# Moving the low parts of two weight blocks behind the activations' work, and finishing the norms' column halves one by one

## The chip, the cores and the metric

One core of a Trainium2 chip runs the whole program in one launch. The metric is device time in microseconds from launch to end, the median of several executions. Engines named below: PE is TensorE (matmuls and transposes), PEld its weight loads, DVE is VectorE, ACT is ScalarE, POOL is GpSimd, SP is the queue that issues nearly all of the loads.

## The reference, cut to what matters

256 tokens of width 1024 pass through four layers (first block), then through two more of another kind, which the change does not touch. The part of a layer that the change touches:

```python
        y = mixer(h)                                  # attention of one of three kinds, ends in @ w_out
        x = x + rmsnorm(y, g[1])
        y = sqrelu_mlp(rmsnorm(x, g[2]), mlp_w1[i], mlp_w2[i])   # square(relu(h @ w1)) @ w2, 1024 -> 4096 -> 1024
        x = x + rmsnorm(y, g[3])
        x = x + jax.nn.sigmoid(x @ ple_gate_w[i]) * (p[i] @ ple_w[i])
```

All of it is in fp32. The kernel keeps that accuracy with three passes of a faster type: each operand a is split in a high part (rounded to `fp32r`) and a low part (a minus the high part), and a product is high x high + low x high + high x low.

## The kernel before, in words

**Pieces of weights.** A weight block of 512 rows by 512 columns (1 MB) is loaded by SP into a buffer `raw`; ACT casts it into `whi` (the high part); DVE subtracts in two instructions of 128 x 1024 to give `wlo` (the low part, `rest`, L289). There are four buffers of each of the three names. A `raw` buffer is free for the next load only when the low part has been taken from it. `piece` does cast and subtraction together (cast at L270); `high` and `low` do them apart (cast at L277). Column block 0 of the MLP's first weights and of the gate's weights is made by `high` and `low`; each consists of two pieces, k = 0 and k = 1.

**Activations.** `transpose_in` turns 128 tokens of x into operands with the features on the partitions: four transposes on PE for each column half, then ACT writes the high part (`xTh`) and DVE the low part (`xTl`, both L423).

**End of a mixer (`first_layer`).** `mixed` multiplies the mixer's output by w_out, tokens 0 to 127 first (`y`), then tokens 128 to 255 (`y1`, through `begin` and `end`). DVE forms `gg` and `xg` (L2192, L2196) from x and the norms' weights. `enter(y, h)` finds the norm of y (squares on ACT, a chain of small DVE instructions), and for each column half multiplies (L2202) and adds (L2203) to give xg[h], the unnormalised input of the MLP. The order in the program is: enter(y, 0); the end of y1; the cast of the small weight `ple_w`; `high` and `low` of the MLP's first block; transposes of xg[0]; `ple_in` (transposes of p); enter(y1, 1); `ple_proj` (p @ ple_w on PE, its results kept in one of the `raw` buffers until the layer ends); transposes of xg[1]; then `update`, which adds the normed y to x itself (L2208, L2209, eight instructions); then the MLP. The MLP's column block 0 goes through `mm_a4` (L342): all of its high x high matmuls, then all low x high, then all high x low. After it the blocks alternate between `mm_a` and the product with w2 (`mm_b`); the w2 pieces of block 0 and the w1 pieces of block 1 come through the four `raw` buffers in that order.

**End of a layer.** `post_norm` norms the MLP's output Y[h] and adds it to x[h], again multiply (L457) and add (L458) for each column half. The gate's two column blocks `ug` are made by `unit_apart` (block 0) and `unit` (block 1). Then, for h = 0 and 1: transposes of x[h], and the gate matmuls `mm_b`, column block 0 before block 1, in each for k = 0 and k = 1: high x high, low x high, high x low.

**What sets the order.** The program order above is a ranking. The compiler keeps a timeline of its own and gives each engine's queue the highest ranked instruction whose operands are ready in that timeline, some instructions ahead of the one that executes; the queue then runs in that order on the chip. `with self.behind(done)` adds order alone: what is traced inside on the engine of `done` stands behind `done` in that engine's queue, and does not wait for it to end. `self.weighted` is the mixer's last multiplication on DVE. The SP queue is in order too: a load that waits for a buffer holds those behind it.

Of the kernel before, what the change touches and what calls it, by code (L numbers as in the profile page):

```python
# [16 lines left out]
OP = mybir.AluOpType  # L17
# [35 lines left out]
class Net:  # L53
# [239 lines left out]

        return [self.piece(w[k * 512:(k + 1) * 512, c0:c0 + nc_], 4 * k, perm) for k in range(2)]

    def unit_apart(self, w, c0):

        raws = [self.load(w[k * 512:(k + 1) * 512, c0:c0 + 512]) for k in range(2)]
        u = [self.high(raw, 4 * k) for k, raw in enumerate(raws)]
        for p, raw in zip(u, raws):  # L300
            self.low(p, raw)
        return u


# [145 lines left out]
    def post_norm(self, y, g, h, r2):  # L450

        v = self.nc.vector
        r4 = self.small([128, 1], "r4")
        v.tensor_scalar(r4, r2, r2, 1.0 / D, op0=OP.mult, op1=OP.mult)
        r = self.rstd(y, scale=r4, factor=r2)
        for n, yn in zip(HALVES, y):
            v.scalar_tensor_tensor(yn, yn, r, g[:, n], op0=OP.mult, op1=OP.mult)  # L457
            last = v.tensor_add(self.x[h][:, n], self.x[h][:, n], yn)  # L458
        return last


# [1714 lines left out]
    def first_layer(self, i, mix, oT, w_out, after):  # L2176
        nc, v = self.nc, self.nc.vector
        ng = self.a["norm_g"][i]
        xg, r2 = {}, {}
        y, begin, end = self.mixed(mix, oT, w_out)  # L2180
        raws = [self.load(self.a["mlp_w1"][i, k * 512:(k + 1) * 512, :512]) for k in range(2)]
        mT = self.xT_new()
        if i == 3:
            self.pools = ExitStack()
            self.rt = self.pools.enter_context(self.tc.tile_pool(name="rt", bufs=1, reuse_waits="tile"))
        with self.phase(f"mlp{i}", 4, 4):

            g1, g2 = self.bcast(ng[1]), self.bcast(ng[2])
            gg = self.tm()

            with self.behind(self.weighted):
                v.tensor_tensor(gg, g1, g2, OP.mult)  # L2192
                for h in range(2):
                    xg[h] = self.tm()
                    for n in HALVES:
                        v.tensor_tensor(xg[h][:, n], self.x[h][:, n], g2[:, n], OP.mult)  # L2196

            def enter(y, h):
                r = self.rstd(y)
                for n, yn in zip(HALVES, y):  # L2200
                    t = self.t2([128, 512])
                    v.scalar_tensor_tensor(t, yn, r, gg[:, n], op0=OP.mult, op1=OP.mult)  # L2202
                    v.tensor_add(xg[h][:, n], xg[h][:, n], t)  # L2203
                return r

            def update(y, h, r):
                for n, yn in zip(HALVES, y):
                    v.scalar_tensor_tensor(yn, yn, r, g1[:, n], op0=OP.mult, op1=OP.mult)  # L2208
                    v.tensor_add(self.x[h][:, n], self.x[h][:, n], yn)  # L2209
                r = self.rstd([self.x[h]])  # L2210
                r2[h] = self.one([128, 1], f"r2{h}")
                v.tensor_tensor(r2[h], r, r, OP.mult)

            r0 = enter(y, 0)
            y1 = begin()
            for u in range(2):
                end(y1, u)
            pc = self.piece(self.a["ple_w"][i])
            u1 = [self.high(raw, 4 * k) for k, raw in enumerate(raws)]
            with self.behind(self.weighted):  # L2220
                for u, raw in zip(u1, raws):
                    self.low(u, raw)
            self.transpose_in(xg[0], mT, 0)
            pT = self.ple_in(i)
            r1 = enter(y1, 1)
            self.ple_proj(pc, pT)
            last = self.transpose_in(xg[1], mT, 1)
            with self.behind(*last):
                update(y, 0, r0)
                update(y1, 1, r1)  # L2230
            g3 = self.bcast(ng[3])
            Y, last = self.mlp(i, mT, u1)
            if i == 3:
                self.router_loads()
            xT = self.xT_new()
            y = [self.wide(), self.wide()]
            self.post_norm(Y[0], g3, 0, r2[0])
            with self.behind(*last):
                ug = [self.unit_apart(self.a["ple_gate_w"][i], 0)]
            for h in range(2):  # L2240
                last = self.transpose_in(self.x[h], xT, h)
                if h == 0:
                    with self.behind(*last):
                        ug.append(self.unit(self.a["ple_gate_w"][i], 512))
                    self.post_norm(Y[1], g3, 1, r2[1])
                for u in range(2):
                    self.now(self.mm_b(y[h][u], xT, ug[u], h))
        after(lambda h: self.gated(y[h], h, i == 3))
# [133 lines left out]
```

## Time and profile before

| | us |
|---|---|
| median of 3 runs | 2271.1 |
| lowest and highest of them | 2264.89, 2271.54 |
| profiled execution, own time | 2268.48 |
| its span (first to last instruction) | 2266.7 |
| mean granted TensorE clock | 0.973 |

The profiled execution is one more run of the same program; what lies around its span is 1.8 us. In the rows, a line such as "157.57 1.19 PE L308 MATMUL pB<-whi,xTl ... x4 [1.74 <-DVE rx L360]" says: from 157.57 us on, for 1.19 us, PE ran four matmuls of line 308 with these operands into a PSUM buffer, after it had been idle for 1.74 us, which ended with an event that the profile puts down to DVE's line 360.

### The profile page before, as it was taken

How to read it: one execution, taken by the hardware profiler on the slowest of the kernel's cores; microseconds unless marked ns; L12 is line 12 of the kernel's file. 1: busy time of each engine (PE TensorE's matmuls, PEld its weight loads, DVE VectorE, ACT ScalarE, POOL GpSimd, SP SyncE). 2: the span in 40 equal slices, each digit the busy share in tenths (PEclk: the TensorE clock that was granted, in tenths of full speed). 3: DMA queues.
4: the chain of work that ended last, by engine and by line, in shares of the span. 5: the costliest groups of instructions: out<-in, count | busy, mean ns of one | idle time of the engine just before them, and what ended most of it. 6: DMA issues, size and time to landing. Idle time of an engine off the chain costs nothing. (4 is left out here: it accounts for less than half of the span.)

```text
span 2266.7 us, 35540 instructions
## 1 busy us (share of the span) xinstructions
PE 2104.9 (93%) x14072; PEld 1608.8 (71%) x14072; DVE 1346.7 (59%) x2794; ACT 937.4 (41%) x1464; POOL 25.2 (1%) x69
## 2 busy tenths in 40 slices
PE   7989999989999999999999899989898988989897
PEld 5868888976788878788888698978743327864332
DVE  4578767575877665877666787677611027851112
ACT  4545435455543455544445444446411115521111
POOL 0000000000000010000000000000000001000000
PEclk9999999999999999999999999999999998999999
DMA  8527774630587464477564387656599984469995
GB/s 296 182 74 253 268 257 171 212 121 29 191 279 278 169 217 155 173 260 267 202 229 161 87 284 261 215 205 205 225 407 418 420 353 155 152 246 420 418 419 225
DMA packets 246362, 541.67 MB, mean 239 GB/s; under 512 B 27501, under 2 KB 77189, under 8 KB 246181
## 3 DMA queue, kind: packets, MB, share of 16 engines
q1 hardware_dynamic: 242597, 533.98, 65.3%
q10 hardware_dynamic: 3552, 5.24, 0.6%
q8 instruction: 116, 1.90, 0.3%
q14 instruction: 65, 0.53, 0.1%
q0 software_dynamic: 32, 0.02, 0.0%
HBM read 533.36 MB, written 5.83 MB: 238 GB/s over the span
## 5 line engine op out<-in xcount | busy, mean ns | idle before, releaser
L289 DVE TENSOR_TENSOR wlo<-raw,whi 128x1024 fp32r<-128x1024 f32 x476 | 558.5, 1221 | 223.9 <-ACT whi L270 201.8
L270 ACT CAST whi<-raw 128x2048 fp32r<-128x2048 f32 x218 | 411.1, 1907 | 417.9 <-PE pB L308 336.8
L308 PE MATMUL pB<-whi,t 128*128 128x512 f32 x1088 | 308.1, 401 | 4.7 <-ACT t L423 3.2
L308 PE MATMUL pB<-xTl,whi 128*128 128x256 f32 x1600 | 257.0, 285 | 0.0
L308 PE MATMUL pB<-xTh,whi 128*128 128x256 f32 x1600 | 254.9, 288 | 0.4 <-ACT whi L270 0.4
L308 PE MATMUL pB<-xTh,wlo 128*128 128x256 f32 x1600 | 250.2, 284 | 0.0
L308 PEld LDWEIGHTS pB<-whi,t 128*128 128x128 f32 x1088 | 202.0, 191 | 49.0 <-ACT t L423 4.1
L308 PEld LDWEIGHTS pB<-xTh,whi 128*128 128x128 f32 x1600 | 218.8, 193 | 11.8 <-issue 8.6
L308 PEld LDWEIGHTS pB<-xTl,whi 128*128 128x128 f32 x1600 | 223.2, 193 | 5.3 <-issue 2.3
L308 PEld LDWEIGHTS pB<-xTh,wlo 128*128 128x128 f32 x1600 | 217.8, 192 | 2.7 <-issue 1.7
L308 PE MATMUL pB<-wlo,t 128*128 128x512 f32 x544 | 170.9, 395 | 0.0
L308 PE MATMUL pB<-whi,xTh 128*128 128x512 f32 (+1 forms) x512 | 145.0, 409 | 11.4 <-ACT xTh L423 9.3
L308 PE MATMUL pB<-whi,xTl 128*128 128x512 f32 (+1 forms) x512 | 143.5, 402 | 10.1 <-DVE xTl L423 6.7
L308 PE MATMUL pB<-wlo,xTh 128*128 128x512 f32 (+1 forms) x512 | 139.9, 395 | 0.0
L1195 DVE SCALAR_TENSOR_TENSOR adac<-adaw,cs,adac 128x512 f32<-128x512 f32 x168 | 125.8, 749 | 21.5 <-DMA adaw<-in_w_ada_dram 19.0
L1829 PE MATMUL pB<-wlo,t 128*32 128x512 f32 (+1 forms) x1024 | 116.6, 594 | 11.7 <-ACT t L1747 11.7
L1753 DVE SCALAR_TENSOR_TENSOR t<-pB,gs,g 128x512 f32<-128x512 f32 x32 | 24.0, 751 | 166.2 <-PE pB L1829 164.6
L308 PEld LDWEIGHTS pB<-whi,xTh 128*128 128x128 f32 x512 | 95.4, 197 | 37.2 <-ACT xTh L423 15.2
L308 PEld LDWEIGHTS pB<-whi,xTl 128*128 128x128 f32 x512 | 96.9, 198 | 34.6 <-DVE xTl L423 8.7
L308 PEld LDWEIGHTS pB<-wlo,t 128*128 128x128 f32 x544 | 103.0, 189 | 24.1
L1829 PE MATMUL pB<-whi,xg 128*32 128x512 f32 (+1 forms) x1024 | 114.4, 593 | 0.0
L308 PEld LDWEIGHTS pB<-wlo,xTh 128*128 128x128 f32 x512 | 96.0, 194 | 21.6 <-issue 2.7
(384 smaller groups left out, 2375.9 us busy)
## 6 DMA issues: line engine op xcount, KB each, us to landing
raw<-in_mlp_w_dram SPq DMA_DIRECT2D x128, 1024.0 KB
whi<-in_moe_w_up_dram SPq DMA_DIRECT2D x64, 1024.0 KB
wlo<-in_moe_w_down_dram SPq DMA_DIRECT2D x56, 1024.0 KB
adaw<-in_w_ada_dram SPq DMA_DIRECT2D x96, 512.0 KB
raw<-in_moe_w_gate_dram SPq DMA_DIRECT2D x48, 1024.0 KB
raw<-in_da_w_in_dram SPq DMA_DIRECT2D x24, 1024.0 KB
raw<-in_ple_gate_w_dram SPq DMA_DIRECT2D x16, 1024.0 KB
xTl<-in_moe_w_gate_dram SPq DMA_DIRECT2D x16, 1024.0 KB
```

The costliest lines, as they stand in the source:

```text
L270: done = nc.scalar.copy(hi, raw)
L289: last = subtract(lo[:, ks], raw[:, ks], hi[:, ks].bitcast(F32), OP.subtract)
L308: self.last_mm = self.nc.tensor.matmul(ps, l, r, start=start and i == 0, stop=stop and i == n - 1)
L1195: v.scalar_tensor_tensor(acc, t[:, i], self.cs[:, k + i:k + i + 1], acc, op0=OP.mult, op1=OP.add)
L1753: self.nc.vector.scalar_tensor_tensor(t, p, gs, g2[:, n], op0=OP.mult, op1=OP.mult)
L1829: self.last_mm = self.nc.tensor.matmul(out[u][es], xT[:, k0 + k, es], t[:, s, k, c], start=done[u] == 1, stop=done[u] == total[u], tile_po ...
```

## The change

`unit_apart` takes two lists of instructions, `first` and `then`: the casts of the gate's block 0 go behind the one, its subtractions behind the other. The casts stay behind the MLP's last work on ACT. The subtractions, which stood behind the MLP's last work on DVE, now stand behind the last addition of post_norm(Y[0]). In `first_layer` the four subtractions of the MLP's first block leave their place behind the mixer's last multiplication, and stand behind the last evacuation of the transposes of xg[1], ahead of `update`. In `post_norm` and `enter` the second column half's multiplication goes behind the first half's addition in DVE's queue.

```diff
-    def unit_apart(self, w, c0):
+    def unit_apart(self, w, c0, first=(), then=()):
 
         raws = [self.load(w[k * 512:(k + 1) * 512, c0:c0 + 512]) for k in range(2)]
-        u = [self.high(raw, 4 * k) for k, raw in enumerate(raws)]
-        for p, raw in zip(u, raws):
-            self.low(p, raw)
+        with self.behind(*first):
+            u = [self.high(raw, 4 * k) for k, raw in enumerate(raws)]
+        with self.behind(*then):
+            for p, raw in zip(u, raws):
+                self.low(p, raw)
         return u
...
         r = self.rstd(y, scale=r4, factor=r2)
+        last = ()
         for n, yn in zip(HALVES, y):
-            v.scalar_tensor_tensor(yn, yn, r, g[:, n], op0=OP.mult, op1=OP.mult)
-            last = v.tensor_add(self.x[h][:, n], self.x[h][:, n], yn)
+            with self.behind(*last):
+                v.scalar_tensor_tensor(yn, yn, r, g[:, n], op0=OP.mult, op1=OP.mult)
+            last = (v.tensor_add(self.x[h][:, n], self.x[h][:, n], yn),)
         return last
...
             def enter(y, h):
                 r = self.rstd(y)
+                last = ()
                 for n, yn in zip(HALVES, y):
                     t = self.t2([128, 512])
-                    v.scalar_tensor_tensor(t, yn, r, gg[:, n], op0=OP.mult, op1=OP.mult)
-                    v.tensor_add(xg[h][:, n], xg[h][:, n], t)
+                    with self.behind(*last):
+                        v.scalar_tensor_tensor(t, yn, r, gg[:, n], op0=OP.mult, op1=OP.mult)
+                    last = (v.tensor_add(xg[h][:, n], xg[h][:, n], t),)
                 return r
...
             u1 = [self.high(raw, 4 * k) for k, raw in enumerate(raws)]
-            with self.behind(self.weighted):
-                for u, raw in zip(u1, raws):
-                    self.low(u, raw)
             self.transpose_in(xg[0], mT, 0)
...
             last = self.transpose_in(xg[1], mT, 1)
             with self.behind(*last):
+
+                for u, raw in zip(u1, raws):
+                    self.low(u, raw)
                 update(y, 0, r0)
                 update(y1, 1, r1)
...
             y = [self.wide(), self.wide()]
-            self.post_norm(Y[0], g3, 0, r2[0])
-            with self.behind(*last):
-                ug = [self.unit_apart(self.a["ple_gate_w"][i], 0)]
+            normed = self.post_norm(Y[0], g3, 0, r2[0])
+            ug = [self.unit_apart(self.a["ple_gate_w"][i], 0, last, normed)]
```

## Rows read from the trace of the kernel before

**Rows 1.** The page: busy time of an engine, share of the span, instructions.
```profile
PE 2104.9 (93%) x14072; PEld 1608.8 (71%) x14072; DVE 1346.7 (59%) x2794; ACT 937.4 (41%) x1464; POOL 25.2 (1%) x69
```
**Rows 2.** Timeline, layer 0, mixer's end: start, us, engine, line, tiles, [idle before].
```profile
154.49 2.36 DVE L289 TENSOR_TENSOR wlo<-raw,whi 128x1024 fp32r<-128x1024 f32 x2
...
157.57 1.19 PE L308 MATMUL pB<-whi,xTl 128*128 128x512 f32 x4 [1.74 <-DVE rx L360]
...
160.43 1.07 PE L308 MATMUL pB<-wlo,xTh 128*128 128x512 f32 x4
...
161.13 2.35 DVE L289 TENSOR_TENSOR wlo<-raw,whi 128x1024 fp32r<-128x1024 f32 x2
...
164.23 0.63 PE L434 MATMUL pB<-ident,tm 128*128 128x128 f32 x4 [2.29 <-DVE ss L396]
...
166.02 3.52 PE L308 MATMUL pB<-whi,t 128*128 128x512 f32 x8 [0.73 <-ACT t L423]
```
**Rows 3.** Timeline, layer 2, the same stage.
```profile
930.51 1.07 PE L308 MATMUL pB<-wlo,xTh 128*128 128x512 f32 x4
...
930.85 2.36 DVE L289 TENSOR_TENSOR wlo<-raw,whi 128x1024 fp32r<-128x1024 f32 x2
...
933.88 2.13 PE L308 MATMUL pB<-whi,t 128*128 128x512 f32 x8 [0.98 <-ACT t L423]
```
**Rows 4.** Timeline, PE's waits in that stage of layers 1 and 3.
```profile
584.43 0.63 PE L434 MATMUL pB<-ident,tm 128*128 128x128 f32 x4 [2.24 <-DVE ss L396]
...
1284.07 1.21 PE L308 MATMUL pB<-whi,xTl 128*128 128x512 f32 x4 [1.74 <-DVE rx L360]
...
1290.72 0.63 PE L434 MATMUL pB<-ident,tm 128*128 128x128 f32 x4 [2.26 <-DVE ss L396]
```
**Rows 5.** Windows of 2 us: busy time of each engine, then PEclk, DMA share, GB/s.
```profile
168.00:170.00 2.00, 2.00 (x6) 1.51 (x5) 2.00 (x4) 0.00 (x0) 0.00 (x0) 0.56 1.04 424
784.00:786.00 2.00, 2.00 (x11) 1.66 (x10) 1.90 (x6) 2.00 (x2) 0.00 (x0) 1.00 0.00 0
934.00:936.00 2.00, 2.00 (x9) 1.65 (x10) 1.83 (x8) 0.00 (x0) 0.00 (x0) 1.00 0.99 258
1132.00:1134.00 2.00, 2.00 (x7) 1.55 (x6) 1.86 (x9) 2.00 (x3) 0.00 (x0) 0.58 0.00 1
```
**Rows 6.** Timeline, layer 0, from the loads ahead of the MLP to its second block.
```profile
165.28 1.44 SPq L239 DMA_DIRECT2D raw<-in_mlp_w_dram  x3
...
175.77 2.73 DVE L2208 SCALAR_TENSOR_TENSOR pB<-pB,ry,tm 128x512 f32<-128x512 f32 x4
...
182.07 1.91 ACT L270 CAST whi<-raw 128x2048 fp32r<-128x2048 f32 x1 [3.44 <-PE pB L342]
...
182.35 4.00 PE L342 MATMUL pB<-xTh,wlo 128*128 128x256 f32 x32
...
186.23 2.12 PE L308 MATMUL pB<-whi,t 128*128 128x512 f32 x8
```
**Rows 7.** Timeline, layer 1, from the MLP's end to the gate.
```profile
772.74 4.63 DVE L289 TENSOR_TENSOR wlo<-raw,whi 128x1024 fp32r<-128x1024 f32 x4 [5.42 <-ACT whi L277]
...
777.29 0.15 DVE L396 TENSOR_TENSOR ss<-ss 128x1 f32<-128x1 f32 x1
...
781.77 1.22 PE L434 MATMUL pB<-ident,x 128*128 128x128 f32 x8 [1.72 <-DVE x L458]
...
783.15 0.68 DVE L423 TENSOR_TENSOR xTl<-pB,xTh 128x512 fp32r<-128x512 f32 x1
...
783.52 3.72 ACT L270 CAST whi<-raw 128x2048 fp32r<-128x2048 f32 x2
...
784.11 1.07 PE L308 MATMUL pB<-whi,xTl 128*128 128x512 f32 x4
```
**Rows 8.** Timeline, layer 0, the gate's first low x high matmuls.
```profile
371.03 1.08 PE L308 MATMUL pB<-whi,xTl 128*128 128x512 f32 x4
```

## The prediction, written before the changed kernel was run

> **What bounds the kernel now.** I read the page first: PE is busy for 93% of the span and DVE for 59% [rows 1], so a change on DVE is worth time only where PE stands still for it. I then went through the timeline of the stages that the diff touches, the end of the mixer and the start of the gate, in each of the four layers, looked for idle time ahead of PE's rows and asked which DVE instruction had kept it waiting.
>
> At the end of the mixer in layer 0 PE waits twice. At 157.57 it has waited 1.74 us for the low part of a transposed operand, and the row just before that on DVE is a pair of subtractions of 2.36 us; at 164.23 it has waited 2.29 us to transpose the second half of xg[0], behind the second pair at 161.13 [rows 2]. Both pairs are the MLP's low parts, which nothing needs until much later. Layer 3 has the same two waits, and layer 1 the second one [rows 4]. In layer 2 the second pair falls behind both additions, and PE does not wait [rows 3].
>
> These waits have an echo. The first eight matmuls of ple_proj take 3.52 us in layer 0 [rows 2] and 2.13 in layer 2 [rows 3]; the granted clock is 0.56 (nearly all of the stretch at 1.2 GHz) in the one and 1.00 (2.4 GHz) in the other [rows 5]. What PE did before is the difference: from the end of y1 to these matmuls it had 4.52 us with little work in layer 0 (161.50 to 166.02) and 2.30 in layer 2 (931.58 to 933.88) [rows 2, 3].
>
> At the gate of layer 1 DVE does four subtractions from 772.74 to 777.37, and the norm's first addition (ss) stands right behind them; PE then waits 1.72 us for x before it transposes [rows 7]. Layers 2 and 3 repeat this; in layer 0 the wait is about a third of it.
>
> **Mixer's end: four subtractions leave.** With them gone I expect layers 0, 1 and 3 to run as layer 2 does. The first wait goes in layers 0 and 3: 2 x 1.74 = 3.5 us [rows 2, 4]. The stretch from the end of y1 to ple_proj shrinks from 4.52 to 2.30, thus 2.2 us; layers 1 and 3 have the same second wait (2.24 and 2.26) and get the same: 3 x 2.2 = 6.7. The clock should then hold: 3.52 - 2.13 = 1.4 in each, 4.2 in all. What is late next is the chain of y1's norm, but it is hidden by ple_proj in layer 2, so I count nothing. Layer 2 gains nothing. Sum: 14.3 us gained.
>
> **The same four, ahead of update.** They follow the evacuation of xg[1], where update begins today at 175.77, and end 4.7 us later at 180.5; mm_a4 asks for them at 182.35 [rows 6], so mm_a4's first two passes hide them, with 1.9 us to spare. Without that cover they would cost 4.7. Behind them on DVE are the eight instructions of update (four are 2.73 us) and then the low parts of w2's first pieces; x itself is not read for a long time, but update also frees y's four PSUM buffers, which Y's matmuls want at 186.23. By my sum update ends at about that time, perhaps a microsecond later.
>
> The dearer part is the raw buffers. Today both pairs are done before 165.28 and three loads are issued there at once [rows 6]. After the change two of the four buffers are held by the MLP's first block until 178.2 and 180.5, and one holds ple_proj's results, so one load goes early and the third, block 1's first piece, only at 180.6. At the 424 GB/s of a busy window [rows 5] 1 MB takes 2.5 us; with two in flight 5. Its cast (1.91, today at 182.07) would end at 185 to 187.5, and its first use comes behind Y's eight matmuls, at 188.35 [rows 6]. That fits narrowly, and the pieces behind it are later still, since their buffers wait for w2's low parts. Bounds: nothing, or some 2 us a layer. I take 1 in each of four layers: 4 us lost.
>
> **Gate: four subtractions go behind post_norm's last addition.** The norm starts without them: x comes up to 1.72 us earlier, and the transposes with it. I take 1.5 in layers 1 to 3 and 0.7 in layer 0. But the subtractions rank above the evacuation xTl in the program, and they are ready at once, while xTl still waits for PE and ACT. A queue that takes the first ready instruction puts all four ahead of xTl. In layer 1 the second addition ends by 782.3 today, then at 780.8; the four run until 785.4, and xTl (0.68) until 786.1, where today it starts at 783.15. The low x high matmuls start at 786.2 in place of 784.11: 2.1 late. PE can fill with four high x high matmuls of block 1 (0.9 us), since their cast, today at 783.52, ends at about 784 [rows 7]. Net 1.2 lost in each of layers 1 to 3, and 2.1 + 0.8 - 0.9 = 2.0 in layer 0, against 371.03 [rows 8]: 5.6 us. Today these subtractions lie where DVE had been idle for 5.42 us [rows 7]; that cover is what the move gives up. The raw buffers come free later here too, for block 1's second piece and the next layer's first load; neither is asked for within 5 us by my count, so nothing.
>
> Whether the new pause costs the clock is open. Today PE has the same 1.72 us wait in layers 1 and 2; layer 2's next matmuls run at 0.58 and layer 1's at 1.00 [rows 5]. The new pause is longer (about half of 6 us busy). I take two layers that lose it in place of one: 1.4 us lost, with bounds of 1.4 gained (none) and 4.2 lost (all four).
>
> A rule stands behind this last term. The Trainium skill, "TensorE: Matmul & The Clock Gate", section "HAM oscillation — how this bites in real kernels", says that waits between short runs of matmuls throttle the array again, so that each run starts cold. The trace agrees at the end of the mixer in layer 0 and at the gate of layer 2, and not at the gate of layer 1. By the rule alone the term would be 4.2, and the sum 2.8 us higher.
>
> **Halves one by one.** The first half's addition ends one multiplication (2.73 / 4 = 0.7 us) sooner, the second half's when it did. PE needs both halves soon after each other, so I count nothing; bounds are 0.7 gained for each of the eight norms that PE waits on, and 0.1 lost, if an addition directly behind its multiplication starts a little late.
>
> **Sum.** 14.3 - 4 - 5.6 - 1.4 = 3.3 us gained. Against the profiled execution, 2268.48, that is 2265. This execution lies 2.6 us under the median of the runs shown, 2271.1, and within their spread (2264.89 to 2271.54). About 0.3%, 6.8 us, is what a measurement of this kernel can tell from no change.
>
> **Rivals.**
> *xTl goes first at the gate.* If the evacuation stands ahead of the subtractions, or between the two pairs, the gate's start is earlier, and only the high x low matmuls wait. In layer 1: xTl's two parts end at 782.9, the first pair at 785.3, when by today's order 12 matmuls are nearly done, and with the filler 16; I get 0.7 gained for each layer. Then 14.3 - 4 + 2.8 = 13.1 gained, 2255; with the raw buffers costing nothing, 2251. For it: a few instructions are queued ahead, so the order depends on when the compiler thinks xTl ready. Against it: xTl needs a transpose and a cast behind the first addition, and the subtractions need nothing.
>
> *The raw buffers decide: slower.* Place: the start of the MLP, blocks 0 and 1. Block 1's second piece can load only after w2's first low part, which ranks behind update: at about 186 in place of 181. If PE stands still for that delay of 5 us in each of four layers, 20 us go: 14.3 - 7 - 20 = 12.7 lost, 2281. It decides from a loss of 3.5 us a layer (14 in all) on. For it: the loads are issued as buffers come free. Against: PE has the rest of Y's matmuls to do meanwhile.
>
> *The gain at the mixer's end is eaten.* PE may meet the next wait there: y1's norm, or a cast that slips between the two evacuations on ACT. With half of 14.3 gone: 2272, no change.
>
> **Chances.** Forecast 0.56, xTl first 0.18, gain eaten 0.14, raw buffers 0.12. The forecast lies just above the border of "faster" (2264.3), so it gives 0.42 of its weight to faster and nearly all the rest to no change. Together: faster 0.41, within 0.3% 0.47, slower 0.12. The range takes in the first rival with free buffers (2251) and stops short of the slow one's full price: 2250 to 2278.
>
> **What would show it.** Right: in layers 0, 1 and 3 no subtraction between the mixer's evacuations, no PE wait over 1 us there, ple_proj's first eight matmuls at about 2.1 us and a clock of 1.00; four subtractions in a row behind xTl of xg[1], over before mm_a4's last pass; at the gate, four subtractions in a row ahead of xTl, with PE idle ahead of the low x high matmuls for 2 to 3 us. Wrong: xTl ahead of them; a PE wait over 2 us at Y's first matmuls or in block 1; an ACT cast that waits for a raw load there; or a clock still near 0.6 in ple_proj.

## The result, and the profile after

The change makes the kernel slower: 2281.8 us (median of 7, 2278.55 to 2289.82) against 2271.1 (7 runs, 2264.89 to 2274.04), a ratio of 1.0056, 95% interval 1.0039 to 1.0073, which is 12.7 us (the two medians lie 10.7 apart). The forecast was 2265 with a range of 2250 to 2278: wrong in sign, and 4 us outside the range.

The page of the changed kernel, busy time of each engine: PE's work is the same to 1.3 us [rows 1], so what was lost is, on balance, waiting.

```profile
PE 2103.6 (92%) x14072; PEld 1604.2 (70%) x14072; DVE 1347.1 (59%) x2794; ACT 938.1 (41%) x1464; POOL 26.3 (1%) x69
```

To place it I compared the start of the matmul with the same number in both traces (14,072 in each) and took the difference at five marks in each of the four layers: 110 matmuls ahead of mm_a4, mm_a4's first, 300 further on (about block 2 of the MLP), the MLP's end (some 30 matmuls ahead of its last), and 205 further (layer 3: 415), in the next mixer. The table gives each stage's growth in us, summed over the four layers (minus is gained). "Elsewhere" is the rest up to matmul 14,000, in places without an edit: single executions differ there by a few us, so whole kernels are judged by their ratios and the table only says where. The traced executions of e3 and e8 are slow ones among their runs (5.8 and 7.0 us over the median), that of e9 is the fastest of its own (5.7 under). The first expectations give the change's three stages as 17 to 18 us gained, 19 lost and 19 to 21 lost, where these marks give 14.9, 16.4 and 17.8.

```
kernel                                mixer's end  MLP's first blocks  rest of MLP  gate and next start  elsewhere   in all
the change                              -14.9            16.4              1.3            17.8             -5.9      14.7
  layers 0, 1, 2, 3                 -4.6 -4.2 0 -6.2  2.4 3.5 0.5 9.9                4.6 4.9 3.4 4.9
e1   MLP part alone                     -14.4            17.3             -1.5            -3.0              2.2       0.6
e2   gate part alone                      1.2             1.7             -0.2            12.8             -0.3      15.2
e3   halves alone                         3.7            -2.3             -0.1             8.5             -0.8       9.0
e4   change, pw in its own buffer         2.0             0.2              4.9            21.7             -4.4      24.4
e5   MLP's low parts 3 us earlier       -16.5             1.9              0.3            -1.6              1.2     -14.7
e6   e2, Y[1]'s norm first                1.6             0.2             -0.2             7.3             -7.5       1.4
e7   before, gate's low parts last        0.1             0.8             -3.2             9.6             -4.5       2.8
e8   e1, router's loads later           -14.3            16.8              5.1            -0.6              4.7      11.7
e9   e5, router's loads spread          -15.8            -4.7             -2.7            -0.1             -0.9     -24.2
e10  e5, gate's low parts split         -15.9            -0.1             -2.7             2.1             -1.0     -17.6
e11  e9 and e10                         -14.9            -4.4             -2.7             4.1             -2.4     -20.3
e12  change, two places mended          -14.3             2.9             -2.7            22.4             -2.9       5.4
e13  change without the halves          -15.4            12.6             -0.2            12.2             -4.1       5.1
e14  e12 without the halves             -15.2             2.4              1.9             7.3             -6.0      -9.6
```

**The mixer's end** went as forecast. Timeline of the changed kernel, layer 0, and the window behind it (columns as in [rows 5]):

```profile
157.61 1.23 PE L436 MATMUL pB<-ident,tm 128*128 128x128 f32 x8
...
160.05 2.43 PE L310 MATMUL pB<-whi,t 128*128 128x512 f32 x8 [0.77 <-ACT t L425]
```

```profile
160.00:162.00 2.00, 1.95 (x7) 1.23 (x8) 1.87 (x8) 0.00 (x0) 0.00 (x0) 1.00 0.79 205
```

All eight transposes of xg[0] run together where PE had stopped for 2.29 us between the halves, and ple_proj's first eight matmuls take 2.43 us at a granted clock of 1.00, against 3.52 at 0.56 [rows 2, 5].

**The MLP's start** loses it again. Timeline, layer 0:

```profile
159.26 0.41 SPq L239 DMA_DIRECT2D raw<-in_mlp_w_dram  x1
...
168.56 4.62 DVE L289 TENSOR_TENSOR wlo<-raw,whi 128x1024 fp32r<-128x1024 f32 x4
170.99 18.61 SPq L239 DMA_DIRECT2D raw<-in_mlp_w_dram  x6
...
176.07 1.91 ACT L270 CAST whi<-raw 128x2048 fp32r<-128x2048 f32 x1 [6.46 <-DMA raw<-in_mlp_w_dram]
...
184.54 0.74 PE L310 MATMUL pB<-xTh,wlo 128*128 128x256 f32 x4 [1.30 <-DVE wlo L289]
```

Before, three loads were issued at once at 165.28 [rows 6], 9.3 us ahead of mm_a4's first matmul (174.58). Now one is, and the next goes at 170.99, when the first pair of subtractions has freed a buffer, 3.6 us after mm_a4 has begun at 167.37. ACT stands 6.46 us for it, and PE later waits 1.30 us for block 1's low parts. Layers 1 and 2 have the same wait (1.46 and 1.27). Layer 3 is the worst, and there PE waits for something else. Its timeline, then two windows (columns as in [rows 5]):

```profile
1299.98 0.37 SPq L239 DMA_DIRECT2D raw<-in_mlp_w_dram  x1
...
1301.73 4.62 DVE L289 TENSOR_TENSOR wlo<-raw,whi 128x1024 fp32r<-128x1024 f32 x4
...
1304.94 1.91 ACT L270 CAST whi<-raw 128x2048 fp32r<-128x2048 f32 x1 [3.96 <-DMA raw<-in_mlp_w_dram]
...
1306.56 2.20 SPq L229 DMA_DIRECT2D tm<-mod  x2
...
1308.86 19.34 SPq L239 DMA_DIRECT2D raw<-in_mlp_w_dram  x6
...
1316.67 1.90 ACT L270 CAST whi<-raw 128x2048 fp32r<-128x2048 f32 x1 [9.81 <-DMA raw<-in_mlp_w_dram]
...
1319.10 0.63 ACT L1111 ACTIVATE t<-t 128x512 fp32r<-128x512 f32 x1
...
1319.78 3.78 PE L310 MATMUL pB<-whi,t 128*128 128x512 f32 x8 [7.46 <-ACT t L1111]
```

```profile
1292.00:1298.00 6.00, 5.14 (x26) 4.09 (x24) 5.64 (x17) 2.67 (x6) 0.00 (x0) 1.00 0.58 51
...
1319.00:1321.00 2.00, 1.22 (x3) 1.03 (x4) 2.00 (x3) 1.97 (x3) 0.00 (x0) 0.50 0.61 235
```

Read it from the bottom of the chain. PE stands still for 7.46 us because relu and square (L1110, L1111) are late on ACT. They are late because in ACT's queue a cast stands ahead of them that waits 9.81 us for its load. The first pair of subtractions (half of the 4.62 us from 1301.73 on) had freed that load's buffer at about 1304.0, but on SP the load stands behind the router's small loads and goes only at 1308.86; in layer 0 it went within 0.2 us. Two loads of 512 KB (`tm<-mod`) are issued just ahead of it and another 1 MB right behind it, and its cast starts 7.8 us after its issue, in layer 0 5.1. When PE starts again, its clock is 0.50.

The router's loads also keep the DMA engines 58% busy for 51 GB/s from 1292 to 1298, in packets of under 512 bytes. That did not hold up a 1 MB load issued among them: from 1299.98 to its cast at 1304.94 it took 5.0 us, no longer than in layer 0 without them (170.99 to 176.07).

**The gate.** Timeline, layer 1, against [rows 7]:

```profile
775.08 0.69 DVE L462 TENSOR_TENSOR x<-x,pB 128x512 f32<-128x512 f32 x1
...
776.22 0.60 PE L436 MATMUL pB<-ident,x 128*128 128x128 f32 x4
...
777.20 0.16 DVE L398 TENSOR_TENSOR ss<-ss 128x1 f32<-128x1 f32 x1 [0.76 <-ACT junk L396]
777.27 0.68 DVE L462 TENSOR_TENSOR x<-x,pB 128x512 f32<-128x512 f32 x1
777.87 4.62 DVE L289 TENSOR_TENSOR wlo<-raw,whi 128x1024 fp32r<-128x1024 f32 x4
778.10 0.63 PE L436 MATMUL pB<-ident,x 128*128 128x128 f32 x4 [1.28 <-DVE x L462]
...
781.20 1.19 PE L310 MATMUL pB<-whi,xTh 128*128 128x512 f32 x4 [1.55 <-ACT whi L270]
...
782.53 1.28 DVE L425 TENSOR_TENSOR xTl<-pB,xTh 128x512 fp32r<-128x512 f32 x2
783.27 1.19 PE L310 MATMUL pB<-whi,xTl 128*128 128x512 f32 x4 [0.88 <-DVE xTl L425]
783.73 2.35 DVE L289 TENSOR_TENSOR wlo<-raw,whi 128x1024 fp32r<-128x1024 f32 x2
...
795.14 0.66 PE L436 MATMUL pB<-ident,x 128*128 128x128 f32 x4 [1.20 <-DVE x L462]
...
795.56 3.65 PE L310 MATMUL pB<-whi,xTh 128*128 128x512 f32 x8
```

The first transposes start 5.55 us before 781.77 (the layer itself runs about 3.7 early by then), but four waits follow: 1.28 us for the second half of x, 1.55 for the second block's cast, 0.88 for xTl, which stands behind the four subtractions as forecast, and, twelve us on, 1.20 for x[1], whose norm stands behind those four and the second block's four. Then PE runs its eight matmuls at half clock, 3.65 us.

### The profile page after: what moved, and what is told of

It reads as the page before. It is cut to its first block, busy times and chain, and to the rows that moved or that the text cites. A ratio compares the mean times of both kernels' runs of the same rounds, so it can differ in the third digit from the quotient of the medians.

```text
span 2281.4 us, 35540 instructions
## 1 busy us (share of the span) xinstructions
PE 2103.6 (92%) x14072; PEld 1604.2 (70%) x14072; DVE 1347.1 (59%) x2794; ACT 938.1 (41%) x1464; POOL 26.3 (1%) x69
## 5 line engine op out<-in xcount | busy, mean ns | idle before, releaser
L310 PEld LDWEIGHTS pB<-wlo,xTh 128*128 128x128 f32 x512 | 96.9, 194 | 22.4 <-issue 2.7
```

What stands on the lines that cost most here:

```text
L310: self.last_mm = self.nc.tensor.matmul(ps, l, r, start=start and i == 0, stop=stop and i == n - 1)
```

## The experiments

**One part at a time.** Each takes some hunks of the change and leaves the rest of the kernel as it was. e1, the MLP's low parts:

```diff
-            with self.behind(self.weighted):
-                for u, raw in zip(u1, raws):
-                    self.low(u, raw)
...
             with self.behind(*last):
+                for u, raw in zip(u1, raws):
+                    self.low(u, raw)
                 update(y, 0, r0)
```

e2, the gate's (`unit_apart` as in the change):

```diff
-                ug = [self.unit_apart(self.a["ple_gate_w"][i], 0)]
+            ug = [self.unit_apart(self.a["ple_gate_w"][i], 0, last, normed)]
```

e3, the halves in `post_norm` and `enter`:

```diff
-            v.scalar_tensor_tensor(yn, yn, r, g[:, n], op0=OP.mult, op1=OP.mult)
+            with self.behind(*last):
+                v.scalar_tensor_tensor(yn, yn, r, g[:, n], op0=OP.mult, op1=OP.mult)
```

> The kernel before with one part of the change: the MLP's four low parts move from the mixer's end to a place ahead of update. By the start times of the same matmuls in the two traces, the change gained 17 to 18 us at the mixer's end of layers 0 to 3 and lost 19 us in the first blocks of the MLP. If these two belong to this part alone, it comes out within 3 us of before (2268 to 2274). If the halves that are finished one by one gave a good share of the mixer's gain, this kernel is slower than that, by 4 us or more. My forecast had 10.3 us gained for this part.

> The kernel before with one part of the change: the four subtractions of the gate's first block move behind the last addition of post_norm. By the same comparison of start times the change lost 19 to 21 us between the MLP's end and the end of the gate in layers 0 to 3. If that is this part's, the kernel takes 2288 to 2292. If the halves one by one have a share in it (an addition that stands behind the squares of the other tokens in DVE's queue), it takes 2278 to 2287. My forecast had 7 us lost (2278).

> The kernel before with one part of the change: in post_norm and in enter the second half's multiplication stands behind the first half's addition. My forecast had nothing for it (within 3 us of before). The rival, that a gap between the halves lets instructions of the other tokens' norm into DVE's queue and PE then waits for the second half, makes it slower by 0.5 to 1 us at each gate and gives 0.7 back at some norms: 2268 to 2276.

Ratios: e1 1.0004 (0.9993 to 1.0016), e2 1.0055 (1.0038 to 1.0072), e3 1.0017 (1.0008 to 1.0026). The MLP part is a trade without profit, 14.4 us gained and 17.3 lost; the gate part is all loss, 12.5 us; and the halves, costed at nothing, cost 4. The sum is 17 where the change lost 12.7.

**e4, one raw buffer more.**

```diff
-        self.pw = self.wt("raw", [128, 2, D], F32)
+        self.pw = self.one([128, 2, D], "pw")
```

> The changed kernel, but ple_proj's results lie in a buffer of their own and no longer occupy one of the four raw buffers from the mixer's end to the end of the layer. All else is left. Theory one: the losses at the MLP's start (19 us) and at the gate (19 to 21 us) come from loads that wait for raw buffers which the moved low parts hold; with one buffer more the next load is issued in time, and at least half of the 38 us comes back: 2262 or less. Theory two: the losses come from the place of the subtractions in DVE's queue (ahead of update, ahead of the evacuation at the gate), and the loads that wait are a by-product: then nothing changes, 2278 to 2285.

1.0104 (1.0091 to 1.0118): slower by another 10 us, which neither theory had. By stage both are half right. At the MLP's first blocks the loss falls from 16.4 to 0.2, so there it was buffers; the later start of mm_a4 is not what hides it, since the next load still goes 3.6 us into mm_a4 in layer 0 (173.87), but one more piece is loaded and cast by then (156.59). At the gate it stays, though the second block's two casts run at once and wait for no load (the last row below, layer 1), so there it is DVE's order. And the freed buffer does harm at the mixer's end. Timeline, layers 0 and 1:

```profile
156.59 1.90 ACT L270 CAST whi<-raw 128x2048 fp32r<-128x2048 f32 x1
...
160.57 3.51 PE L310 MATMUL pB<-whi,t 128*128 128x512 f32 x8 [2.14 <-ACT t L425]
...
170.31 4.10 PE L344 MATMUL pB<-xTh,whi 128*128 128x256 f32 x32 [1.62 <-ACT xTh L425]
...
790.12 3.71 ACT L270 CAST whi<-raw 128x2048 fp32r<-128x2048 f32 x2
```

A piece that loads earlier is also cast earlier, and its casts now stand ahead of the evacuations on ACT: PE waits 2.14 and 1.62 us, the clock falls, and the stage's 14.9 us are gone.

**e5, the low parts in a third place.** From before, without their old place; `entered` is enter's last addition:

```diff
             r1 = enter(y1, 1)
+            with self.behind(*self.entered):
+                for u, raw in zip(u1, raws):
+                    self.low(u, raw)
```

> The kernel before with the MLP's four low parts in a third place: behind the last addition of enter(y1, 1), ahead of the evacuations of xg[1] (the change puts them behind these). Gate and halves as before. DVE is idle for 2.1 us there after the change, so the raw buffers come free 3.3 us earlier than after the change, and mm_a4's second pass, which reads xTl, starts 4 us behind its first. If the loss in the MLP's first blocks (20 us in the run of this part alone, of which 10 in layer 3) is the price of the late subtractions, it falls to 8 or less, and the 17 to 18 us at the mixer's end stay: 2256 to 2261. If it is the price of taking them away from the mixer's end at all (the raw buffers are free 6 us later than before in any place behind the second norm), it stays within 3 us of before.

0.9949 (0.9936 to 0.9962): 2254.5 against 2266.55, 11.6 us faster than before. Timeline, layer 0:

```profile
165.14 4.63 DVE L289 TENSOR_TENSOR wlo<-raw,whi 128x1024 fp32r<-128x1024 f32 x4
...
167.57 19.80 SPq L239 DMA_DIRECT2D raw<-in_mlp_w_dram  x6
167.72 4.09 PE L342 MATMUL pB<-xTh,whi 128*128 128x256 f32 x32 [0.29 <-ACT xTh L423]
...
172.50 1.91 ACT L270 CAST whi<-raw 128x2048 fp32r<-128x2048 f32 x1 [2.54 <-DMA raw<-in_mlp_w_dram]
```

The load goes at mm_a4's start and not 3.6 us into it; ACT's wait falls from 6.46 to 2.54 us, and PE's disappears. In layer 3 the first blocks still lose 6.0 us. Counted from mm_a4's first matmul the subtractions start 2.6 us ahead of it and not 1.2 us behind (in e1 as in the change): 3.8 us of place on DVE are the whole difference between a trade without profit and a gain.

**e6 and e7, what costs at the gate.** e6 is e2 with the second block's low parts behind the two multiplications of Y[1]'s norm. e7 is before with the gate's four subtractions behind the evacuations of x[0] (second diff).

```diff
                     self.post_norm(Y[1], g3, 1, r2[1])
+                    with self.behind(self.scaled):
+                        for p, raw in zip(ug[1], b1):
+                            self.low(p, raw)
```

```diff
                 last = self.transpose_in(self.x[h], xT, h)
                 if h == 0:
+                    with self.behind(*last):
+                        for p, raw in self.later:
+                            self.low(p, raw)
```

> The gate part alone (2281.5 against 2268.8), and in addition the low parts of the gate's second column block stand behind the two multiplications of post_norm(Y[1]). In the run of the gate part alone eight subtractions, 9.3 us, stand ahead of these multiplications on DVE, and PE waits for x[1]. If that wait and the low clock behind it are the larger share of the loss, the loss shrinks by 1.5 to 3 us a layer: 2270 to 2276. If the evacuation xTl behind the first four subtractions is the larger share, it stays above 2278.

> The kernel before, with the gate's four subtractions behind the evacuations of x[0] (before: ahead of the norm; the change: between the norm and the evacuations). The norm starts without them, xTl goes first, and the raw buffers come free later than in the change. If the loss at the gate is the late xTl, most of it goes: 2265 to 2272. If it is the raw buffers (the second piece of the gate's second block, whose load is issued behind the first low part), it is as large as in the gate part alone or larger: 2281 or more. If it is DVE's length (the subtractions stand ahead of post_norm(Y[1]) here too), it lies between, 2274 to 2281.

e6 1.0013 (1.0004 to 1.0022): 9.6 of 12.5 us come back. e7 1.0023 (1.0014 to 1.0032): 7.3 come back, and its 2272.6 lies between the ranges given for the late xTl (to 2272) and for DVE's length (from 2274). Layers 1 to 3 of this stage lose 9.3 us in e2, 2.3 in e6 and 2.9 in e7: either repair, Y[1]'s norm early or xTl early, gives back most, so the two costs are no separate sums. The raw buffers as main cause fall with e7, which frees them last of all. Timelines of e2 and of e6, layer 1, at x[1]:

```profile
798.11 0.66 PE L436 MATMUL pB<-ident,x 128*128 128x128 f32 x4 [1.50 <-DVE x L460]
...
800.38 2.87 PE L310 MATMUL pB<-whi,xTh 128*128 128x512 f32 x6 [0.21 <-ACT xTh L425]
```

```profile
795.96 1.04 PE L436 MATMUL pB<-ident,x 128*128 128x128 f32 x8
...
797.29 2.11 PE L310 MATMUL pB<-whi,xTh 128*128 128x512 f32 x8 [0.30 <-ACT xTh L425]
```

Layer 0 still loses 4.9 us in e6, and half of it, 4.21 less 1.81, lies at the start of the next mixer, where six subtractions stand ahead of an evacuation. Timeline of before, then of e6:

```profile
388.41 6.89 DVE L289 TENSOR_TENSOR wlo<-raw,whi 128x1024 fp32r<-128x1024 f32 x6
...
397.15 0.74 PE L308 MATMUL pB<-whi,xTl 128*128 128x256 f32 x4 [1.81 <-DVE xTl L423]
```

```profile
391.51 6.89 DVE L289 TENSOR_TENSOR wlo<-raw,whi 128x1024 fp32r<-128x1024 f32 x6
...
400.26 1.22 PE L310 MATMUL pB<-whi,xTl 128*128 128x256 f32 x4 [4.21 <-DVE xTl L425]
```

**e8 and e9, layer 3's small loads.** e8 is e1 with the router's loads behind the load of block 1's last piece; e9 is e5 with them a few at a time between the loads of blocks 1 to 5.

```diff
             if i == 3:
-                self.router_loads()
+                with self.behind(self.mark):
+                    self.router_loads()
```

```diff
             u2 = [self.piece(w2[j * 512 + k * 256:j * 512 + (k + 1) * 256, :], 2 * k) for k in range(2)]
+            if i == 3 and 1 <= j <= 5:
+                with self.behind(self.loading):
+                    next(self.few), next(self.few)
```

> The MLP part alone (2269.5 against 2268.8), and in addition, in layer 3, the small loads for the router stand on SP behind the load of the last piece of the MLP's block 1. In the run of the MLP part alone layer 3 lost 10.5 us there, four times what layer 0 lost, and the small loads stood on SP ahead of the MLP's. If that order on SP is the cause, 6 to 8 us come back: 2261 to 2264. If layer 3's loss has another cause (the late low parts themselves), it stays at 2268 to 2271.

> The run with the low parts behind enter(y1, 1) (12 us faster than before), and in addition, in layer 3, the router's small loads go one by one between the MLP's loads of blocks 1 to 5. In that run layer 3 still lost 6.6 us in the MLP's first blocks while layers 0 to 2 lost next to nothing; the DMA engines were more than half busy with 12,080 packets of under 512 bytes there, at 16 to 20 GB/s, and a weight load issued in the middle of them at 1277.83 was awaited until 1283.08. If those packets are the cause, 4 to 6 us come back: 16 to 18 us faster than before. If the small loads cost as much wherever they stand (with the router's loads behind block 1 the loss came up in the block behind it), it stays at 10 to 13 us faster.

e8 1.0031 (1.0021 to 1.0042): not what I expected. In layer 3 the first blocks lose 7.1 us in place of 10.6, but the rest of the MLP loses 3.0 in place of nothing: the wait moved. In the first blocks PE now waits 6.14 us, at 1346.38, for `adac`. DVE makes it late, since it has waited 10.24 us for weights (`adaw`) whose loads stand on SP among the router's and behind them (1333.58, 1335.05):

```profile
1338.83 1.54 DVE L1197 SCALAR_TENSOR_TENSOR adac<-adaw,cs,adac 128x512 f32<-128x512 f32 x2 [10.24 <-DMA adaw<-in_w_ada_dram]
```

Other layers, where only the compiler's order changed, lost some us too, which I did not trace. e9 0.992 (0.9908 to 0.9933), 18 us faster than before: spread, the small loads cost layer 3's first blocks nothing (0.7 us gained, 6.0 lost in e5), so their place is the cause. That it is their packets, as I had written, is not shown: in e5 a load among them took 5.25 us from issue to cast (1277.83 to 1283.08), in layer 0 without them 4.93 (167.57 to 172.50). What e9 removes is the place of the weight loads behind them on SP and behind the two loads of `mod`; it does not separate these. Timeline, layer 3, of e5, then of e9:

```profile
1277.83 0.58 SPq L239 DMA_DIRECT2D raw<-in_mlp_w_dram  x1
...
1283.08 1.91 ACT L270 CAST whi<-raw 128x2048 fp32r<-128x2048 f32 x1 [2.04 <-DMA raw<-in_mlp_w_dram]
...
1296.46 3.78 PE L308 MATMUL pB<-whi,t 128*128 128x512 f32 x8 [4.09 <-ACT t L1107]
```

```profile
1285.49 1.91 ACT L270 CAST whi<-raw 128x2048 fp32r<-128x2048 f32 x1 [0.92 <-PE pB L342]
...
1289.61 2.02 PE L308 MATMUL pB<-whi,t 128*128 128x512 f32 x8
```

**e10 and e11, the gate's subtractions split.** e10 is e5 with the first piece's pair ahead of the norm, the second's behind the evacuations, and the second block's as in e6; e11 adds e9's loads.

```diff
-                ug = [self.unit_apart(self.a["ple_gate_w"][i], 0)]
+                ug = [self.unit_apart(self.a["ple_gate_w"][i], 0, 1)]
```

> The run with the low parts behind enter(y1, 1) (12 us faster than before), and in addition at the gate: the first piece's two subtractions stay ahead of the norm, the second piece's two go behind the evacuations of x[0], and those of the second column block behind the two multiplications of post_norm(Y[1]). The norm starts some 1.7 us earlier in layers 1 to 3 and 0.6 in layer 0, xTl goes first, and Y[1]'s norm stands behind two subtractions in place of eight. If the gate's loss was the place of the subtractions and not that they were moved, this gains 3 to 5 us: 15 to 17 us faster than before. If PE meets another wait (x[1], or the second piece's low part), nothing is gained: 10 to 13 us faster.

> The two additions together: if each gives what its theory says, 19 to 22 us faster than before; if neither does, 10 to 13.

e10 0.9925 (0.9911 to 0.994), e11 0.9916 (0.9901 to 0.993). e10 is in its expected range. e11 reaches the lower edge of its range (19 us), but e11 and e9 can't be told apart, so the two additions do not add in full, and by stage the gate doesn't carry e10's gain: layers 2 and 3 gain 4.5 us there and layers 0 and 1 lose 6.7. e11, 2249.1 us against 2268.85, has the lowest median of all; e9 has nearly the same with less.

**e12 to e14, why the parts don't add.** e12 is the change with e5's place and e6's order (their diffs above); e13 is the change without the halves (e1 and e2 together), e14 is e12 without them (e5 and e6 together).

> The changed kernel with two of its places altered: the MLP's low parts behind enter(y1, 1) in place of behind the evacuations of xg[1], and the low parts of the gate's second block behind the two multiplications of post_norm(Y[1]). The gate's four subtractions and the halves stay as in the change. By the runs of the parts alone (12 faster, 3 slower, 4 slower) the sum is 5 us faster than before, 3 to 8. If the parts' losses are separate only because each was run alone, and together the gate's waits come back, it is no faster than before.

> The changed kernel without the halves that are finished one by one (the MLP's and the gate's moves alone). Alone the three parts were 1, 12.5 and 4 us slower than before, 17 in sum, and the change itself was 12.7 slower. If the halves add their 4 us in the change too, this is 8 to 10 us slower than before. If they add nothing where the gate's subtractions have moved (the wait for the second half then lies beside another wait), it is 12 to 14 us slower, as the gate part alone.

> The run with two altered places (7 us slower than before, where the sum of the parts was 5 faster), without the halves one by one. If the halves are what broke the sum (in layer 1's gate PE waits 1.28 us for the second half of x, which stands behind the squares of the other tokens, and the casts and evacuations follow late), this is 7 to 10 us faster than before. If the MLP's early place and the gate's move do not add, it stays between 3 faster and 7 slower.

e12 1.0032 (1.0022 to 1.0041), e13 1.0037 (1.0024 to 1.0051), e14 0.9951 (0.9937 to 0.9964). e12 missed its range (3 to 8 us faster). e13 is in its range for halves that add their 4 us, and e14 is 1 us faster than its range for the halves as cause. The halves cost 4 us in the change (12.7 to 8.4, with intervals that overlap) and 18 in the mended one (7.3 slower to 11.1 faster). At the gate and the next start the table has 22.4 with them and 7.3 without. They are what broke the sum.

## Why the prediction was wrong

**Mixer's end: right.** Forecast 14.3 us gained, 14.9 in the trace, none of it in layer 2. That the next late thing, y1's norm, is hidden held too.

**"I take 1 in each of four layers: 4 us lost": the step that failed first.** It measured 16.4 (17.3 alone). The mechanism was the one named, two buffers held by the low parts and one by ple_proj's results, and e4 and e5 show it; the size was wrong. In layers 0 to 2 PE waits for block 1's low parts themselves, and the 2.4, 3.5 and 0.5 us lost are together about the upper bound of 2 a layer. One reason is the load's price: 5.1 us from issue to cast in layer 0, and not the 2.5 that the busy window's rate gave. Layer 3 lost 9.9. The sum took the time at which a matmul needs the piece; there the in-order queues decide: the load stands on SP behind others, its cast stands on ACT ahead of relu and square, and so a late load stops work that needs nothing of it. In layer 3 I had not read what else SP carries. The prediction's own sign of being wrong, an ACT cast that waits for a raw load, came in layer 0 (6.46 us). The rival "the raw buffers decide" named place and price (20 us), and its 2281 is the time that came; but it kept the gate at 7 us, so the agreement in the sum is partly luck.

**Gate, 5.6 + 1.4 lost: too small by 5 (12.5 alone).** xTl behind the four subtractions came as forecast, 0.88 us of wait behind the filler; in e6 the first 40 matmuls of the gate lose 1.8, 0.9, 0.9 and 1.0 us in the four layers, where the sum had 2.0 and three times 1.2. "The raw buffers come free later here too ... so nothing" held for the loads as such (e4), though the second block's second cast did slip behind its load in e2. What the sum left out is what else stands behind the subtractions on DVE: Y[1]'s norm, whose wait e6 removes.

The clock's term was taken as two layers in four losing it once, in place of one. In e2 it is two: layer 1 at x[1], layer 2 at the first matmuls with xTl (2.08 us). In the change it is all four: layers 0 and 3 at the first matmuls with xTl, layers 1 and 2 at x[1] (eight matmuls in 3.65 and 3.29 us), a wait that the term did not have. Layer 2 had lost it before too, so at the price of 1.4 us that is 4.2 lost in place of 1.4. Timeline of the changed kernel, layers 0 and 3:

```profile
369.05 2.07 PE L310 MATMUL pB<-whi,xTl 128*128 128x512 f32 x4 [0.85 <-DVE xTl L425]
...
1502.59 2.08 PE L310 MATMUL pB<-whi,xTl 128*128 128x512 f32 x4 [0.87 <-DVE xTl L425]
```

Four of these take 1.07 us at full clock [rows 7]. On this point the rule of the Trainium skill that the prediction set beside its term ("TensorE: Matmul & The Clock Gate", section "HAM oscillation — how this bites in real kernels") gives the change's count, four, but not the places. After the same three waits (1.28, 1.55 and 0.88 us; 1.29, 1.54 and 0.87 in layer 3) the first matmuls with xTl took 1.19 us in layers 1 and 2 and 2.08 in layer 3. Why layer 3 alone fell there is open.

**Halves at nothing, bounds 0.7 gained and 0.1 lost each: wrong side.** Ordering the second multiplication behind the first addition opens a gap of which another chain makes use: ss of Y[1] is put between the halves, waits 0.76 us for ACT, and holds the second addition. The bound counted the two instructions and not who may step in between. In e3 something else steps in, rx of Y[1] in layer 1; PE waits 0.76 us for the second half, and the clock falls, where before four of these matmuls took 1.07 us [rows 7]. Timeline of e3, layer 1:

```profile
782.09 0.63 PE L434 MATMUL pB<-ident,x 128*128 128x128 f32 x4 [0.76 <-DVE rt L362]
...
783.84 1.91 PE L308 MATMUL pB<-whi,xTl 128*128 128x512 f32 x4
```

In e3's traced execution the loss is 8.5 us, 4.9 at the gates and the rest nearly all at the mixer behind layer 2; by the ratio the whole kernel loses 4. In the change it is 12.7 less 8.4, also 4.

**One thing stays open:** why the halves cost 18 us in e12 and 4 in the change. The traces say where it is. Up to the gate's hundredth matmul e12 has lost 9.1 us and e14 8.6, summed over the layers; from there to the last mark e12 loses 13.3 more and e14 gains 1.3. That is the next mixer's start, where six subtractions stand ahead of xTl as in e6. Timeline, layer 1, of e12, then of e14:

```profile
804.92 1.19 PE L310 MATMUL pB<-whi,xTl 128*128 128x512 f32 x4 [3.33 <-DVE xTl L425]
```

```profile
804.30 1.20 PE L310 MATMUL pB<-whi,xTl 128*128 128x512 f32 x4
```

In the change PE has lost 20.0 us by the gate's hundredth matmul, and in layers 0 to 2 it waits at most 0.69 us for this xTl: it comes later itself. Why the six subtractions end later against PE in e12 than in e14 no run shows.

## What to carry to other kernels

Cost a moved instruction by the queues: what stands behind it on its own engine, what its late buffer release keeps back, and which in-order queue will then stand at the transfer. A place only 3.8 us earlier, in the last idle stretch before the buffers are wanted, made 12 us of gain out of no change. An order that only parts two neighbours is not free either: something else moves in between.

## What was not expected of the hardware

The router's loads are 12,104 packets of under 512 bytes. They held the DMA engines 58% busy while these moved 51 GB/s, and yet a 1 MB load issued among them took no longer than one without them: 4.96 us from issue to cast (1299.98 to 1304.94) against 5.08 in layer 0 (170.99 to 176.07). Both are twice the 2.5 us that the 424 GB/s of a busy window [rows 5] give for 1 MB. What the small loads did cost is place in SP's queue: the next 1 MB load, whose buffer was free at about 1304.0, went at 1308.86.
